# Sixteen transposes of the identity at four places, and the last product's activations 128 bytes lower

## The chip, the cores and the metric

The kernel runs on one core of a Trainium2 chip, alone. The metric is the device time of one execution, in microseconds (us). The median of three runs of the kernel before is 845.64 us (844.99 to 845.87). Weights are float32 in HBM; with the other inputs 139 MB are read. A core has TensorE (PE, matrix products; its weight loads are shown apart as PEld), VectorE (DVE), ScalarE (ACT), GpSimd (POOL) and SyncE (SP, which issues the weight transfers). TensorE multiplies a stationary operand, loaded first, with a moving operand that is streamed past it; here stationary blocks are 128 x 128, and 256 or 512 columns move.

## The reference, cut to what matters

Two transformer blocks on one sequence of 256 tokens with 1024 features. The first has a stick-breaking attention, an RWKV-7 mixer and a gated feed-forward of width 2816; the second a dilated attention with a short convolution, a cross attention to a memory of 256 rows, and a squared-ReLU feed-forward of width 4096.

```python
def first_block(x, ...):
    h = rms_norm(x, norm_mix_pre)                    # o_sb, o_rw, gates from h @ w_in
    x = x + rms_norm(merged @ w_o, norm_mix_post)
    h = rms_norm(x, norm_ffn_pre)
    f = (silu(h @ w_ffn_gate) * (h @ w_ffn_up)) @ w_ffn_down
    return x + rms_norm(f, norm_ffn_post)

def second_block(x, mem, ...):
    x = x + hybrid_mixer(rms_norm_2(x, g_mix), w_in, conv_w, g_attn_out, g_conv_out, w_out)
    x = x + memory_cross_attention(rms_norm_2(x, g_xattn), rms_norm_2(mem, g_mem), ...)
    x = x + squared_relu_mlp(rms_norm_2(x, g_mlp), w_up, w_down)
    return rms_norm_2(x, g_final)
```

## The kernel before, in words

**Products.** Weights come in slabs of 128 x 1024 elements (512 KB). For each slab SP issues a transfer into `wraw` (3 buffers), ACT rounds it to `whi` (4 buffers, L193) and DVE takes the rest, `wlo` (4 buffers, L194). The activations lie in memory as such a pair too (`xh`, `xl`; `yh`, `yl`; `fh`, `fl`; `ah`, `al`). A product of a 128 x 128 weight block with 256 tokens is three matmuls into one accumulator: hi with hi, weights' hi with activations' lo, weights' lo with activations' hi. A slab is 24 matmuls with 256 moving columns, one straight behind the other.

**Roles.** In most products the weights are stationary and the activations move (`block`, L258, written `mm<-xh,whi`: the moving operand stands first). In the groups with `tok` (the values of the memory, `kv(4)` to `kv(7)`, and two groups of `w_in_2`) and in the last product, `w_down_2`, it is the other way round: the activations are stationary and the weights move, in `w_down_2` with 512 columns at a time (`tokens`, L273).

**Places in memory.** A tile's byte address in its partition is set by the order of the pools, and `shift` (L121) puts a dummy tile of so many bytes ahead. In the built program `whi` and `wlo` lie at multiples of 512 bytes; `xh`, `xl`, `yh`, `yl`, `fh`, `fl`, the cross attention's output `xoh`, `xol` and the memory's `memh`, `meml` and keys `kT` at 192 modulo 512 (from `PHASE = 192`). `ah` and `al`, the stationary operand of `w_down_2`, lie at 320 modulo 512, behind a shift of 832 - 192 = 640 bytes.

**Sums of squares.** Each norm needs the sum of squares over the features, which is over partitions. `rstd_sum` makes it with one float32 matmul of a 128 x 128 tile of ones, `ssum` (two passes in the trace), into the first 256 columns of a PSUM bank; ACT then takes a logarithm and an exponential (L156). It is placed in the stream of products: for the first feed-forward behind the first four slabs (`together` calls `between` after the first block of each of four groups), for the dilated attention as the last step of the woven side work, for the convolution in `conv_norm`, ahead of `kv(4)`. Two other norms go through `rstd_tok` (one column for each token, `rtok`).

**Order.** Each engine takes its instructions in the order in which the code issues them. `together` runs the first halves (512 rows) of four groups, then `between`, then the second halves. `weave` runs one step of a generator ahead of each slab. Transposes go through TensorE as matmuls with the identity (`n.c("ident")`, 128 columns), as `turn` in `mlp`, `pt` in `hybrid` and `cross`, `tr` in the first block.

Of the kernel before, what the change touches and what calls it, by code (L numbers as in the profile page):

```python
# [17 lines left out]
P = 128  # L18
T = 256
D = 1024  # L20
# [12 lines left out]
PHASE = 192  # L33
# [59 lines left out]
class Net:  # L93
# [183 lines left out]
        self.nc.scalar.copy(hi, src)  # L277
        self.nc.vector.tensor_sub(lo, src, hi.bitcast(F32))

    def rstd(self, pool, src, width, tag):  # L280

        return self.rstd_sum(pool, [self.squares(pool, src)], width, tag)

    def sumsq(self, pool, s, acc):
        sq = pool.tile([P, 2, T], F32, tag="t2", name="sq", bufs=self.t2)
# [4 lines left out]
        self.nc.vector.tensor_add(a2, acc, sq)  # L290
        return a2

    def rstd_sum(self, pool, parts, width, tag, square=None):

        ps = self.ax("ssum")
        for i, p in enumerate(parts):
            self.mm(ps[:, :T], self.ones, p, start=i == 0)
        lg = pool.tile([P, T], F32, tag="t1", name="lg", bufs=1)
        r = pool.tile([P, T], F32, tag=tag, name=tag)
        self.act(lg, ps[:, :T], AF.Ln, bias=self.eps, scale=1.0 / width)  # L300
        self.act(r, lg, AF.Exp, scale=-0.5)
        if square is not None:
            self.act(square, lg, AF.Exp, scale=-1.0)
        return r
# [49 lines left out]
def staggered(count, *stages, apart=1):  # L354


    n = len(stages)
    for s in range(count + n - 1):
        for k, stage in zip(range(n - 1, -1, -1), stages):
            if 0 <= s - k < count:  # L360
                stage(s - k)
        for _ in range(apart):
            yield


def pair(t):
    return t.rearrange("p (o t) -> p o t", o=1).to_broadcast([P, 2, T])


def pairs(t):  # L370
    return [t[:, i:i + 2, :] for i in range(0, t.shape[1], 2)]
# [674 lines left out]
def plain_add(n, w, hi, lo, between=None):  # L1046

    for g, ps in enumerate(n.together([(w, g) for g in range(4)], hi, lo, between)):
        n.nc.vector.tensor_add(n.x[:, 2 * g:2 * g + 2, :], ps, n.x[:, 2 * g:2 * g + 2, :])


def ffn(n, tmp, wide, filler):
    nc, tc = n.nc, n.tc
    with tc.tile_pool(name="ffn", bufs=1, reuse_waits="tile") as pool:
        rs = []
        banks = n.together(FFN_FIRST, n.xh, n.xl, lambda: rs.append(
            pair(n.rstd_sum(tmp, [n.squares(tmp, pairs(n.x))], D, "rs"))))
        r = rs[0]
        n.table("silu_and_others")
        fh = pool.tile([P, FF // P, T], F32R, name="fh")  # L1060
        fl = pool.tile([P, FF // P, T], F32R, name="fl")
        for g in range(FF // 256):
            pg = banks[2 * g] if g < 2 else n.group("w_ffn_gate", g, n.xh, n.xl)
            s = tmp.tile([P, 2, T], F32, tag="t2", name="s", bufs=n.t2)
            nc.vector.tensor_mul(s, pg, r)
            n.act(s, s, AF.Silu)
            pu = banks[2 * g + 1] if g < 2 else n.group("w_ffn_up", g, n.xh, n.xl)
            m = tmp.tile([P, 2, T], F32, tag="t2", name="m", bufs=n.t2)
            nc.vector.tensor_mul(m, pu, r)
            nc.vector.tensor_mul(m, m, s)  # L1070
            n.split(m, fh[:, 2 * g:2 * g + 2, :], fl[:, 2 * g:2 * g + 2, :])
        n.table("natural_log_exp_and_others")
        branch_add(n, tmp, wide, "w_ffn_down", fh, fl, "norm_ffn_post", filler, "g_mix_2")
# [30 lines left out]
def hybrid(n, tmp, kv):  # L1104
    nc, tc = n.nc, n.tc
    with ExitStack() as ctx:
        pool = ctx.enter_context(tc.tile_pool(name="hyb", bufs=1, reuse_waits="tile"))
# [3 lines left out]
        rs = []  # L1111
# [16 lines left out]
        at = pool.tile([P, NP, T], F32, name="at")  # L1128
# [40 lines left out]

        def dilated():  # L1170
            yield from staggered(NP, values, turned, scores, apart=2)
            ra = n.rstd(tmp, pairs(at), 512, "ra")
            n.normed(tmp, pairs(at), ra, "g_attn_out_2", yh, yl)
            yield

        n.weave(dilated())
        for g in range(2):
            ps = n.group("w_in_2", 4 + g, n.xh, n.xl, tok=True)
# [6 lines left out]
        cv = pool.tile([P, NP, T], F32, name="cv")  # L1185
        nc.vector.memset(u[:, :, 0:2], 0.0)
        for g in range(2):
            ps = n.group("w_in_2", 6 + g, n.xh, n.xl)
            nc.vector.tensor_mul(bg[:, 2 * g:2 * g + 2, :], ps, r)
        for g in range(2):  # L1190
            ps = n.group("w_in_2", 8 + g, n.xh, n.xl)
            nc.vector.tensor_mul(cg[:, 2 * g:2 * g + 2, :], ps, pair(r2))
        for g in range(2):
            gg = slice(2 * g, 2 * g + 2)
            ps = n.group("w_in_2", 10 + g, n.xh, n.xl)
# [8 lines left out]
        n.unweave()  # L1204

        def conv_norm():
            rc = n.rstd(tmp, pairs(cv), 512, "rs")
            kv(4, n.ax("kv").rearrange("p (c t) -> p c t", c=2))
            n.normed(tmp, pairs(cv), rc, "g_conv_out_2", yh[:, NP:, :], yl[:, NP:, :])

        plain_add(n, "w_out_2", yh, yl, conv_norm)


def cross(n, tmp, kT, vm, kv):
    nc, tc = n.nc, n.tc
    with ExitStack() as ctx:
        pool = ctx.enter_context(tc.tile_pool(name="xat", bufs=1, reuse_waits="tile"))
        oh = pool.tile([P, KC, T], F32R, name="xoh")
        ol = pool.tile([P, KC, T], F32R, name="xol")
        n.scaled(pairs(n.x), "g_xattn_2", n.xh, n.xl)  # L1220
        rs = []
# [72 lines left out]
        n.weave(attention())  # L1294
        kv(6)
        kv(7)
        plain_add(n, "w_o_mem_2", oh, ol)
        n.unweave()


def mlp(n, tmp, out):
    nc, tc = n.nc, n.tc
    with ExitStack() as ctx:
        pool = ctx.enter_context(tc.tile_pool(name="mlp", bufs=1, reuse_waits="tile"))
        n.shift(pool, 832 - PHASE)
        ah = pool.tile([P, 32, T], F32R, name="ah")
        al = pool.tile([P, 32, T], F32R, name="al")
        n.scaled(pairs(n.x), "g_mlp_2", n.xh, n.xl)
        gf = pool.tile([P, D], F32, name="gf")
        r2 = pool.tile([P, 2], F32, name="r2")  # L1310
        xt = pool.tile([P, 2, D], F32, name="xt")

        def norm():
            n.rstd_tok(pool, [n.squares(tmp, pairs(n.x))], D, square=r2)

        def turned():

            for f in range(2):
                pt = n.ax("turn")
                for i in range(4):  # L1320
                    nc.tensor.transpose(pt[:, i * P:(i + 1) * P],
                                        n.v("g_final_2", 4 * f + i).to_broadcast([P, P]), n.c("ident"))
                nc.scalar.copy(gf[:, f * 512:(f + 1) * 512], pt)
                yield
            for t in range(2):
                for f in range(2):
                    pt = n.ax("turn")
                    for i in range(4):
                        nc.tensor.transpose(pt[:, i * P:(i + 1) * P],
                                            n.x[:, 4 * f + i, t * P:(t + 1) * P], n.c("ident"))  # L1330
                    nc.scalar.copy(xt[:, t, f * 512:(f + 1) * 512], pt)
                    yield

        banks = n.together([("w_up_2", g) for g in range(4)], n.xh, n.xl, norm)
        n.weave(turned())
        for g in range(16):
            ps = banks[g] if g < 4 else n.group("w_up_2", g, n.xh, n.xl)
            a = tmp.tile([P, 2, T], F32, tag="t2", name="a", bufs=n.t2)
            nc.scalar.activation(a, ps, AF.Relu)
            m = tmp.tile([P, 2, T], F32, tag="t2", name="m", bufs=n.t2)  # L1340
            nc.vector.scalar_tensor_tensor(m, ps, 0.0, a, op0=ALU.max, op1=ALU.mult)
            n.split(m, ah[:, 2 * g:2 * g + 2, :], al[:, 2 * g:2 * g + 2, :])
        n.unweave()
        o = pool.tile([P, 2, D], F32, name="o")
        st = pool.tile([P, 2, 4], F32, name="fst")
        for g in range(2):
            gg = slice(g * 512, (g + 1) * 512)
            for t, ps in enumerate(n.tokens("w_down_2", g, ah, al)):
                y = xt[:, t, gg]
                nc.vector.scalar_tensor_tensor(y, ps, r2[:, t:t + 1], y, op0=ALU.mult, op1=ALU.add)  # L1350
                sq = tmp.tile([P, 512], F32, tag="t2", name="sq", bufs=n.t2)
                nc.scalar.activation(sq, y, AF.Square, accum_out=st[:, t, g:g + 1])
                nc.vector.tensor_mul(o[:, t, gg], y, gf[:, gg])
        for t in range(2):
            s = st[:, t, :]
            nc.vector.tensor_add(s[:, 2:3], s[:, 0:1], s[:, 1:2])
            n.act(s[:, 3:4], s[:, 2:3], AF.Ln, bias=n.eps, scale=1.0 / D)
            n.act(s[:, 3:4], s[:, 3:4], AF.Exp, scale=-0.5)
            for f in range(2):
                oo = o[:, t, f * 512:(f + 1) * 512]  # L1360
                if f:
                    nc.vector.tensor_scalar(oo, oo, s[:, 3:4], None, op0=ALU.mult)
                else:
                    nc.scalar.activation(oo, oo, AF.Copy, scale=s[:, 3:4])
                nc.sync.dma_start(out[t * P:(t + 1) * P, f * 512:(f + 1) * 512], oo)
# [85 lines left out]
```

## Time and profile before

| what | value |
| --- | --- |
| median of 3 runs | 845.64 us |
| the profiled execution | 845.12 us |
| its span, first to last instruction | 843.4 us |
| PE busy | 818.9 us, 97% |
| PEld busy | 777.1 us, 92% |
| DVE, ACT busy | 565.0 us (67%), 464.5 us (55%) |
| DMA traffic | 142.88 MB, 169 GB/s mean |

The profiled execution's own time is 1.7 us above its span. PE is busy nearly everywhere, but its matmuls overlap (one is shown as 0.28 us long while the next begins 0.11 to 0.12 us after it), so the share of busy time doesn't tell how fast the products run; the distance between two starts does. Where the text below speaks of a pace, it is that distance, in ns.

### The profile page before, as it was taken

The page shows a single profiled execution, that of the slowest core. Times are in us where ns is not written, and L with a number is a line of the kernel's source. Part 1 is how long each engine was busy: PE and PEld are TensorE (multiplying, and loading weights), DVE is VectorE, ACT ScalarE, POOL GpSimd, SP SyncE. Part 2 cuts the span into 40 slices and gives each one's busy share as a digit, 9 for nine tenths or more (in the row PEclk, how much of TensorE's full clock was granted, in tenths as well). Part 3 has the DMA queues.
Part 4 walks back from the last instruction along what each step waited for, and adds up shares of the span by engine and source line. Part 5 has one row for each costly group of instructions (what it writes and reads, how often), then busy time and mean ns, then how long its engine had stood idle before and what let it go on. Part 6 is the DMA issues. An engine that isn't in the chain of part 4 may idle for free.

```text
span 843.4 us, 15763 instructions
## 1 busy us (share of the span) xinstructions
PE 818.9 (97%) x6508; PEld 777.1 (92%) x6508; DVE 565.0 (67%) x790; ACT 464.5 (55%) x714; POOL 5.7 (1%) x18
## 2 busy tenths in 40 slices
PE   5999998999999999999999999999999999999996
PEld 5898987999999999999999998999999999988884
DVE  6958689455978776666544876689676676654543
ACT  6587355643577654445444656457455575553432
POOL 0001001000000000000000000000000000000000
PEclk9999999999999999999999999999999999999998
DMA  8444433543464755555566464455534555555551
GB/s 289 141 150 152 141 127 119 163 148 99 136 245 147 228 189 185 194 181 191 167 192 184 155 209 146 147 180 193 179 100 155 194 177 178 198 188 186 194 181 51
DMA packets 44632, 142.88 MB, mean 169 GB/s; under 512 B 8977, under 2 KB 9745, under 8 KB 44305
## 3 DMA queue, kind: packets, MB, share of 16 engines
q1 hardware_dynamic: 43840, 139.25, 50.9%
q10 hardware_dynamic: 720, 2.63, 0.8%
q8 instruction: 51, 0.84, 0.4%
q14 instruction: 21, 0.16, 0.1%
HBM read 139.17 MB, written 2.69 MB: 168 GB/s over the span
## 4 chain that ended last, share of the span: by engine, by line
PE 81%; DVE 9%; ACT 4%; DMA 3%; issue 2%; DVEq 0%; ACTq 0%; SPq 0%
PE mm L258 59%; PE mm L273 11%; DVE wlo L194 3%; PE pz L273 2%; ACT whi L193 1%; DMA mraw<-in_mem 1%; PE rw L258 1%; PE po L273 1%; PE px L273 1%; PE mgnh L273 1%; PE ssum L273 1%; PE nv L273 1%; DVE prw L747 1%; PE kv L258 1%; DVE xl L326 1%
## 5 line engine op out<-in xcount | busy, mean ns | idle before, releaser
L194 DVE TENSOR_TENSOR wlo<-wraw,whi 128x1024 fp32r<-128x1024 f32 x254 | 308.2, 1215 | 191.0 <-ACT whi L193 190.2
L193 ACT CAST whi<-wraw 128x1024 fp32r<-128x1024 f32 x254 | 264.6, 1044 | 282.8 <-PE mm L258 162.5
L258 PE MATMUL mm<-xh,whi 128*128 128x256 f32 x1120 | 316.5, 283 | 0.0
L258 PE MATMUL mm<-xh,wlo 128*128 128x256 f32 x1120 | 313.4, 280 | 1.9 <-DVE wlo L194 1.9
L258 PE MATMUL mm<-xl,whi 128*128 128x256 f32 x1120 | 313.4, 280 | 0.0
L258 PEld LDWEIGHTS mm<-xh,wlo 128*128 128x128 f32 x1120 | 212.1, 189 | 3.2 <-DVE wlo L194 2.9
L258 PEld LDWEIGHTS mm<-xh,whi 128*128 128x128 f32 x1120 | 210.9, 188 | 3.7 <-issue 2.1
L258 PEld LDWEIGHTS mm<-xl,whi 128*128 128x128 f32 x1120 | 210.7, 188 | 0.9 <-issue 0.6
L273 PE MATMUL mm<-wlo,ah 128*128 128x512 f32 x128 | 50.6, 395 | 0.0
L273 PE MATMUL mm<-whi,al 128*128 128x512 f32 x128 | 50.6, 395 | 0.0
L273 PE MATMUL mm<-whi,ah 128*128 128x512 f32 x128 | 50.6, 395 | 0.0
L258 PE MATMUL mm<-fh,whi 128*128 128x256 f32 x176 | 49.5, 281 | 0.0
L258 PE MATMUL mm<-fl,whi 128*128 128x256 f32 x176 | 49.5, 281 | 0.0
L258 PE MATMUL mm<-fh,wlo 128*128 128x256 f32 x176 | 49.5, 281 | 0.0
L258 PEld LDWEIGHTS mm<-fh,wlo 128*128 128x128 f32 x176 | 33.8, 192 | 0.0
L258 PEld LDWEIGHTS mm<-fh,whi 128*128 128x128 f32 x176 | 33.0, 188 | 0.0
L258 PEld LDWEIGHTS mm<-fl,whi 128*128 128x128 f32 x176 | 33.0, 188 | 0.0
L273 PEld LDWEIGHTS mm<-whi,al 128*128 128x128 f32 x128 | 24.1, 188 | 5.8
L273 PEld LDWEIGHTS mm<-wlo,ah 128*128 128x128 f32 x128 | 24.1, 188 | 5.8
L273 PEld LDWEIGHTS mm<-whi,ah 128*128 128x128 f32 x128 | 24.1, 188 | 5.7
L258 PE MATMUL rw<-gh,whi 128*128 128x256 f32 x48 | 14.9, 310 | 8.6 <-ACT whi L193 8.6
L258 PE MATMUL mm<-memh,whi 128*128 128x256 f32 x64 | 18.5, 288 | 0.0
(352 smaller groups left out, 1377.4 us busy)
## 6 DMA issues: line engine op xcount, KB each, us to landing
wraw<-in_w_up SPq DMA_DIRECT2D x32, 512.0 KB, 3.3
wraw<-in_w_down SPq DMA_DIRECT2D x32, 512.0 KB, 3.3
wraw<-in_w_in SPq DMA_DIRECT2D x24, 512.0 KB, 4.1
wraw<-in_w_ffn_gate SPq DMA_DIRECT2D x22, 512.0 KB, 3.4
wraw<-in_w_ffn_up SPq DMA_DIRECT2D x22, 512.0 KB, 3.3
wraw<-in_w_ffn_down SPq DMA_DIRECT2D x20, 512.0 KB, 3.6
wraw<-in_w_gate SPq DMA_DIRECT2D x16, 512.0 KB, 3.3
wraw<-in_w_kv_mem SPq DMA_DIRECT2D x16, 512.0 KB, 3.3
```

Of the source, the lines that this page charges most:

```text
L193: nc.scalar.copy(hi[:, :w], raw[:, :w])
L194: nc.vector.tensor_sub(lo[:, :w], raw[:, :w], hi[:, :w].bitcast(F32))
L258: self.nc.tensor.matmul(ps[:, c, :], lhsT, rhs, start=first, stop=last, skip_group_check=True)
L273: self.nc.tensor.matmul(out, lhsT, rhs, start=start, stop=stop, skip_group_check=True)
L326: self.nc.vector.scalar_tensor_tensor(lo[:, k, :], s[:, j, :], g, hi[:, k, :].bitcast(F32), op0=ALU.mult, op1=ALU.subtract)
L747: nc.vector.tensor_mul(pr, left[:, r:r + 4, :].rearrange("p r (o i) -> p r o i", o=1).to_broadcast([P, 4, 16, 16]), right.rearrange("p (o ...
```

## The change

At three of the eight sums of squares, `rstd_sum` is called with `turned=True` and issues four transposes of the identity into the unused second half of the bank of the sum, behind its matmul. In the cross attention's output product, four such transposes go into a bank of their own between the first and the second halves. Nothing reads what they write. The shift in `mlp` is 512 bytes in place of 640, so `ah` and `al` (and `gf`, `xt`, `o` and others behind them) lie 128 bytes lower: `ah` and `al` at 192 modulo 512.

```diff
-    def rstd(self, pool, src, width, tag):
+    def rstd(self, pool, src, width, tag, turned=False):
 
-        return self.rstd_sum(pool, [self.squares(pool, src)], width, tag)
+        return self.rstd_sum(pool, [self.squares(pool, src)], width, tag, turned=turned)
...
+    def turns(self, ps):
+
+        for i in range(4):
+            self.nc.tensor.transpose(ps[:, T + i % 2 * P:T + (i % 2 + 1) * P], self.c("ident"), self.c("ident"))
+
-    def rstd_sum(self, pool, parts, width, tag, square=None):
+    def rstd_sum(self, pool, parts, width, tag, square=None, turned=False):
 
         ps = self.ax("ssum")
         for i, p in enumerate(parts):
             self.mm(ps[:, :T], self.ones, p, start=i == 0)
+        if turned:
+            self.turns(ps)
...
-            pair(n.rstd_sum(tmp, [n.squares(tmp, pairs(n.x))], D, "rs"))))
+            pair(n.rstd_sum(tmp, [n.squares(tmp, pairs(n.x))], D, "rs", turned=True))))
...
-            ra = n.rstd(tmp, pairs(at), 512, "ra")
+            ra = n.rstd(tmp, pairs(at), 512, "ra", turned=True)
...
-            rc = n.rstd(tmp, pairs(cv), 512, "rs")
+            rc = n.rstd(tmp, pairs(cv), 512, "rs", turned=True)
...
-        plain_add(n, "w_o_mem_2", oh, ol)
+        plain_add(n, "w_o_mem_2", oh, ol, lambda: n.turns(n.ax("turns")))
...
-        n.shift(pool, 832 - PHASE)
+        n.shift(pool, 512)
```

On PE in the first feed-forward, at the sum behind the first four slabs (`xh` is the activations, `whi` and `wlo` the weights, `sqa` the squares, `mm_3225` the first group's accumulator, back for its second half), before:

```order
L258 MATMUL mm_3228<-xl_77,whi_3260 128x256
L258 MATMUL mm_3228<-xh_76,wlo_3261 128x256
L273 MATMUL ssum_3364<-sqa_3361,ones_61 128x256 [waits DVE_49]
L258 MATMUL mm_3225<-xh_76,whi_3290 128x256 [waits Activation_49]
L258 MATMUL mm_3225<-xl_77,whi_3290 128x256
```

and after:

```order
L258 MATMUL mm_3228<-xl_77,whi_3260 128x256
L258 MATMUL mm_3228<-xh_76,wlo_3261 128x256
L273 MATMUL ssum_3364<-sqa_3361,ones_61 128x256 [waits DVE_49]
L296 MATMUL ssum_3364<-cst_58 128x128 x4
L258 MATMUL mm_3225<-xh_76,whi_3290 128x256 [waits Activation_49]
```

The four transposes stand between the sum and the next product and wait for nothing of their own; the same holds at the two other sums. On PE in the cross attention's output product, between its first and second halves (`xoh`, `xol` the activations), before:

```order
L258 MATMUL mm_7441<-xol_6863,whi_7497 128x256
L258 MATMUL mm_7441<-xoh_6862,wlo_7498 128x256
L258 MATMUL mm_7438<-xoh_6862,whi_7527 128x256
L258 MATMUL mm_7438<-xol_6863,whi_7527 128x256
L258 MATMUL mm_7438<-xoh_6862,wlo_7528 128x256
```

and after:

```order
L258 MATMUL mm_7453<-xol_6875,whi_7509 128x256
L258 MATMUL mm_7453<-xoh_6874,wlo_7510 128x256
L296 MATMUL turns_7613<-cst_58 128x128 x4
L258 MATMUL mm_7450<-xoh_6874,whi_7539 128x256
L258 MATMUL mm_7450<-xol_6875,whi_7539 128x256
```

Four transposes more, and nothing else moved: the rows of the other engines, and what each of them waits on, are the same in both programs.

## Rows read from the trace of the kernel before

**Rows 1.** The page: span, busy TensorE, granted clock in 40 slices (tenths).

```profile
span 843.4 us, 15763 instructions
...
PE 818.9 (97%) x6508; PEld 777.1 (92%) x6508; DVE 565.0 (67%) x790; ACT 464.5 (55%) x714; POOL 5.7 (1%) x18
...
PEclk9999999999999999999999999999999999999998
```

**Rows 2.** The page: the chain that ended last, by engine and by line.

```profile
PE 81%; DVE 9%; ACT 4%; DMA 3%; issue 2%; DVEq 0%; ACTq 0%; SPq 0%
PE mm L258 59%; PE mm L273 11%; DVE wlo L194 3%; PE pz L273 2%; ACT whi L193 1%; DMA mraw<-in_mem 1%; PE rw L258 1%; PE po L273 1%; PE px L273 1%; PE mgnh L273 1%; PE ssum L273 1%; PE nv L273 1%; DVE prw L747 1%; PE kv L258 1%; DVE xl L326 1%
```

**Rows 3.** Windows, PE: stretch, sum, busy (x matmuls), granted clock, DMA share, GB/s.

```profile
290.00:460.00 170.00, 170.00 (x1445) 1.00 0.59 186
546.00:567.00 21.00, 21.00 (x181) 1.00 0.58 186
569.00:573.50 4.50, 4.50 (x40) 1.00 0.62 217
575.00:596.00 21.00, 21.00 (x180) 1.00 0.62 198
645.00:666.00 21.00, 21.00 (x180) 1.00 0.52 176
695.00:745.00 50.00, 50.00 (x444) 1.00 0.58 192
747.00:833.00 86.00, 86.00 (x370) 1.00 0.50 164
```

**Rows 4.** Timeline of PE, first feed-forward: start us, duration us, instruction; its last product.

```profile
288.10 0.28 PE L258 MATMUL mm<-xh,wlo 128*128 128x256 f32 x1
288.22 0.59 PE L273 MATMUL ssum<-sqa,ones 128*128 128x256 f32 x2
288.46 0.47 PE L258 MATMUL mm<-xh,whi 128*128 128x256 f32 x1
288.77 0.28 PE L258 MATMUL mm<-xl,whi 128*128 128x256 f32 x1
288.88 0.28 PE L258 MATMUL mm<-xh,wlo 128*128 128x256 f32 x1
...
463.78 0.28 PE L258 MATMUL mm<-fh,wlo 128*128 128x256 f32 x1
```

**Rows 5.** Timeline of PE: the last transposes of `mlp`, and `w_up_2` behind them.

```profile
693.72 0.28 PE L258 MATMUL mm<-xh,wlo 128*128 128x256 f32 x1
693.84 0.60 PE L1329 MATMUL turn<-cst,x 128*128 128x128 f32 x4
694.20 0.36 PE L258 MATMUL mm<-xh,whi 128*128 128x256 f32 x1
...
694.51 0.28 PE L258 MATMUL mm<-xh,wlo 128*128 128x256 f32 x1
...
745.87 0.28 PE L258 MATMUL mm<-xh,wlo 128*128 128x256 f32 x1
```

**Rows 6.** Windows, PE: just ahead of transposes in the first block, and behind them.

```profile
55.00:64.00 9.00, 9.00 (x78) 1.00 0.60 198
65.60:68.50 2.90, 2.90 (x28) 1.00 0.51 171
```

**Rows 7.** Timeline of PE, cross attention: where the stationary operand changes.

```profile
609.53 0.28 PE L258 MATMUL mm<-whi,meml 128*128 128x256 f32 x1
...
610.10 0.28 PE L258 MATMUL mm<-whi,memh 128*128 128x256 f32 x1
...
629.64 0.28 PE L258 MATMUL mm<-xoh,whi 128*128 128x256 f32 x1
...
630.35 0.28 PE L258 MATMUL mm<-xoh,whi 128*128 128x256 f32 x1
```

**Rows 8.** Waits of ACT: who waited for whom, us in total, times, longest.

```profile
ACT whi L193 <- PE mm L258: 162.5, 116, 4.7
```

## The prediction, on record before the kernel ran

> **What bounds the kernel now.** I read the page first: PE is busy for 97% of the 843.4 us, at the granted clock's full level (2.4 GHz) in every slice but the last [rows 1]; the chain of waits is 81% PE, and 70% of it are the slab products on two lines [rows 2]. So the kernel ends when its products end, and the question is how fast one follows the other. Weights don't limit that: ACT waits 162.5 us in all for PE to give back a `whi` buffer [rows 8], so slabs stand ready ahead of PE.
>
> Then I took the distance between starts from the timeline of PE, and found **two paces** for the same matmul at the same clock. Behind the sum of squares of the first feed-forward, 1486 steps lie between 288.77 and 463.78 us (62 slabs' worth, 1488 matmuls, counted from the second) [rows 4]: 175.01 / 1486 = 117.8 ns. Behind the last transposes of `mlp`, 453 steps lie between 694.51 and 745.87 (19 slabs, 456 matmuls, counted from the third) [rows 5]: 51.36 / 453 = 113.4 ns. Shape, roles and places modulo 512 are the same in both. The windows show that a pace lasts until something interrupts the products: 1445 matmuls in 170 us, 181 in 21, 180 in 21, 180 in 21 are all the slow one, 444 in 50 us is the fast one (a window counts the two that began just ahead of it, too) [rows 3]. The difference is 4.4 ns a matmul.
>
> What chooses the pace is the restart. The slow stretches that the change is about begin behind a sum of squares or, in the cross attention, behind a value product. Four or more 128-column transposes straight ahead of products are followed by the fast pace in all ten places of this trace that are long enough to tell (at 65, 72, 532 and 634 us, and six within `mlp`), also where the pace ahead of them was slow: 78 in 9 us before, 28 in 2.9 us after [rows 6], which is 118 and 112 ns without the two early ones. Without transposes the restart goes either way.
>
> **The change part by part.**
>
> A. The first feed-forward. If the four transposes leave the products at the fast pace up to the next sum at 463.9 us, 1484 steps gain 4.4 ns each: 6.5 us. Cost: four transposes and the restart behind them. In `mlp`, the transposes take 693.84 to 694.20, 0.36 us, and the restart to the third product's start 0.31 us [rows 5]; the sum's own restart, which now falls away, takes 288.46 to 288.88, 0.42 us [rows 4]. That adds 0.36 + 0.31 - 0.42 = 0.25 us; the step from the sum's second pass to the first transpose isn't in the trace and may cost up to the sum's own restart gap, 0.31 - 0.12 = 0.19 us more. I take 0.35, the middle of 0.25 to 0.45. Net: 6.2 us less. Weights can follow: `w_up_2` runs the fast pace on the same slabs with 192 GB/s against 186 now [rows 3]. The sum's readers on ACT wait at most those 0.4 us longer; DVE needs their result a slab later, PE (through a bank that DVE frees) four slabs later.
>
> B. The dilated attention's sum. Its stretch runs slow from 545 to 568 us [rows 3], 190 steps: 0.84 - 0.35 = 0.5 us less.
>
> C. The convolution's sum. Behind it come 48 matmuls of `kv(4)`, activations stationary (40 in 4.5 us, slow), then 192 with the weights stationary (180 in 21 us, slow) [rows 3]. The only place where such a change of roles met the fast pace without an interruption lost it: from 629.64 to 630.35 six steps take 0.71 us, 118 ns [rows 7]. So I count 46 steps, 0.2 us, against 0.35: 0.15 us more. If the pace holds it is 238 steps, 1.05 - 0.35 = 0.7 us less.
>
> D. The cross attention. The transposes stand alone, at slow pace, with 192 slow matmuls behind them (180 in 21 us) [rows 3]: 0.85 us gained. In `mlp` three steps with transposes between take 693.72 to 694.51, 0.79 us, where three plain ones take 0.34 [rows 5]: 0.45 us. Net 0.4 us less.
>
> E. The last product. It runs 370 matmuls in 86 us [rows 3], 233 ns for 512 columns (1.7 began early). No row shows this product with its operands elsewhere; the bounds come from the 256-column rows doubled: twice the fast pace is 226.7 ns, twice the slow one 235.5. So today's 233.3 is near the slow pace. The place moves the stationary operand to 192 modulo 512 with the moving one at 0, the same relation as in `kv(6)`; there the products come out of a fast stretch (their moving operand at 192, too) and stay fast: from 609.53 to 610.10 five steps in 0.57 us, 114 ns [rows 7]. The last product follows a fast stretch in the same way [rows 5]. I take the fast value, by that nearest row: 383 x (233.3 - 226.7) = 2.5 us less. The ends kept for the range: if a matmul's excess over 512 columns at 2.4 GHz (213.3 ns) is no larger than the fast pace's over 256 (113.4 - 106.7 = 6.7 ns), 220 ns, 5.1 us less; twice the slow pace, 0.8 us more.
>
> Sum: 6.2 + 0.5 - 0.15 + 0.4 + 2.5 = 9.45 us less. The profiled execution took 845.12 us, 0.5 us under the median of the runs: 845.12 - 9.45 = 835.7, and against the median 845.64 - 9.45 = **836.2 us**. Nothing of it is given back later: what DVE and ACT do behind each of these stretches starts from PE's results.
>
> A page speaks against A to E at once. The Trainium skill, "TensorE: Matmul & The Clock Gate", Part 2, says that loading the next weights doesn't take read bandwidth from the running matmul; by that rule neither a restart nor a place in memory could set the pace, and only the costs would remain. The trace disagrees as far as it goes, with 117.8 and 113.4 ns for one shape at one clock [rows 4, 5].
>
> **The rivals.**
>
> R1. The last product's place does nothing (its pace is set within its first steps, not by the place): A to D stay, E is 0: 838.7 us. For it: its start already follows a fast stretch and is slow all the same [rows 3, 5]. Against: the relation of the operands there is another than in `kv(6)`.
>
> R2. The pace is lost on the way. In A it must hold over 62 slabs and the change from `xh` to `fh`; the fast stretch of `mlp` held over 19 [rows 5]. Lost halfway, A gives 2.9 instead of 6.2: 839.5 us with E, 842.0 without.
>
> R3. The sum, not the transposes, sets the pace, or the pace isn't chosen by restarts at all (this is also what the page's rule would make of it): A to D cost 3 x 0.35 + 0.45 = 1.5 us and give nothing. 847.1 us, or 844.6 with E. For it: no row has a sum and transposes in a row. Against: a slow stretch ahead of transposes didn't matter [rows 6].
>
> R4. The other side: the new place hurts the last product. Moving and stationary operand meet at the change of roles at the same place modulo 512, and if each of the 384 weight loads then holds up its matmul, it costs 384 times the stall. It decides from 9.45 - 2.5 = 6.95 us, 18 ns a matmul, a pace over 251 ns. The nearest row is 4.4 ns a weight load (slow against fast), a quarter of it; at 25 ns it would be 838.7 + 9.6 = 848.3 us.
>
> **How the numbers follow.** Forecast 0.45; R1 0.22; R2 0.15; R3 0.13 (0.06 with E, 0.07 without); R4 0.05. About 0.2%, 1.7 us, is what a measurement of this kernel can tell from no change: 843.9 to 847.3. Faster: forecast, R1, R2 and a little of R3, 0.84; same: R3, 0.11; slower: R4 and the worst of R3, 0.05. The range: its low end takes E at 220 ns, 836.2 - 2.6 = 833.6, and C held would lie there too; the high end takes R1 and R2 in, 842.0. R3 and R4 are left out.
>
> **What would show it.** In the changed kernel's timeline: behind the first feed-forward's transposes 24 matmuls take 2.72 us, not 2.83, up to 457 us or so (A); the same at 539 to 560 (B) and behind the cross attention's transposes (D); behind `kv(4)` the pace goes back to 118 (C); the last product's 370 matmuls take 84 us, not 86 (E). The three sums' restarts are 0.25 to 0.45 us longer. I am wrong if the pace behind sum and transposes is 118 ns, if the fast pace breaks at a slab whose weights came late, or if the last product's distance isn't between 220 and 235.5 ns.

## The result, and the profile after

The changed kernel takes 837.15 us (median of 4 runs, 835.33 to 838.26) against 845.32 us before (4 runs, 844.06 to 845.87): a ratio of 0.9906, interval 0.9889 to 0.9923, some 8 us less. 836.2 us was forecast, in a range of 833.6 to 842.0. The profiled execution took 837.66 us, its span 835.9.

The page of the changed kernel answers to [rows 1]. It still shows a PE at 97% and the full clock; only the sum of PE's busy time is smaller:

```profile
span 835.9 us, 15795 instructions
...
PE 811.8 (97%) x6524; PEld 771.9 (92%) x6524; DVE 564.8 (68%) x790; ACT 465.7 (56%) x714; POOL 5.7 (1%) x18
...
PEclk9999999999999999999999999999999999999999
```

The windows show where; columns as in [rows 3], stretches moved along with the products:

```profile
291.00:455.00 164.00, 164.00 (x1450) 1.00 0.61 193
541.00:562.00 21.00, 21.00 (x188) 1.00 0.56 190
563.50:568.00 4.50, 4.50 (x40) 1.00 0.61 222
570.00:590.00 20.00, 20.00 (x179) 1.00 0.61 200
640.00:660.00 20.00, 20.00 (x179) 1.00 0.55 180
592.00:602.00 10.00, 10.00 (x87) 1.00 0.58 202
662.00:672.00 10.00, 10.00 (x87) 1.00 0.58 197
689.00:739.00 50.00, 50.00 (x444) 1.00 0.59 191
742.00:826.00 84.00, 84.00 (x369) 1.00 0.51 166
```

The first feed-forward now has 1450 matmuls in 164 us where it had 1445 in 170; the stretches B and D and the one behind `kv(4)` are fast, too (188 in 21 us for 181, 179 in 20 us for 180 in 21). `kv(4)` itself stays slow, 40 in 4.5 us. The last product has 369 in 84 us for 370 in 86. `w_up_2` behind its transposes is as it was, 444 in 50 us. Two stretches have become slow, which no row ahead of the prediction speaks of: 87 matmuls in 10 us at 592 and 662 us. In the kernel before, the same two ran fast:

```profile
598.00:607.00 9.00, 9.00 (x82) 1.00 0.54 187
...
668.00:677.00 9.00, 9.00 (x82) 1.00 0.57 192
```

The start of the same instruction in the two traces tells where the time went. A row's last column is what its stretch, from the row above, brought:

| instruction on PE | before, us | after, us | difference | change since the row above |
| --- | --- | --- | --- | --- |
| sum of the first feed-forward | 288.22 | 289.19 | +0.97 | +0.97, same code in both |
| sum behind `w_ffn_down` | 463.90 | 458.71 | -5.19 | -6.16 (A) |
| sum of the dilated attention | 544.98 | 539.68 | -5.30 | -0.11 |
| sum of the convolution | 568.02 | 562.32 | -5.70 | -0.40 (B) |
| `rtok` in `w_q_mem_2` | 596.72 | 590.62 | -6.10 | -0.40 (C) |
| first scores of the cross attention | 608.05 | 602.37 | -5.68 | +0.42 |
| its last value product | 639.75 | 634.08 | -5.67 | +0.01 |
| `rtok` in `w_up_2` | 666.61 | 660.54 | -6.07 | -0.40 (D) |
| first transposes in `mlp` | 677.94 | 672.29 | -5.65 | +0.42 |
| first step of the last product | 745.99 | 740.33 | -5.66 | -0.01 |
| its last step | 835.34 | 827.99 | -7.35 | -1.69 (E) |
| end of the span | 843.42 | 835.93 | -7.49 | -0.14 |

The restart of A, to be held against [rows 4]:

```profile
289.07 0.28 PE L258 MATMUL mm<-xh,wlo 128*128 128x256 f32 x1
289.19 0.59 PE L273 MATMUL ssum<-sqa,ones 128*128 128x256 f32 x2
289.62 0.60 PE L296 MATMUL ssum<-cst 128*128 128x128 f32 x4
289.98 0.37 PE L258 MATMUL mm<-xh,whi 128*128 128x256 f32 x1
290.18 0.28 PE L258 MATMUL mm<-xl,whi 128*128 128x256 f32 x1
290.30 0.28 PE L258 MATMUL mm<-xh,wlo 128*128 128x256 f32 x1
```

From the last product ahead of the sum to the third one behind it are 1.23 us where it was 0.78: the four transposes cost 0.45 us here.

### The profile page after: what moved, and what is told of

It is laid out like the page before. It is cut to its first block, busy times and chain, and to the rows that moved or that the text cites. A ratio compares the mean times of both kernels' runs of the same rounds, so it can differ in the third digit from the quotient of the medians.

```text
span 835.9 us, 15795 instructions
## 1 busy us (share of the span) xinstructions
PE 811.8 (97%) x6524; PEld 771.9 (92%) x6524; DVE 564.8 (68%) x790; ACT 465.7 (56%) x714; POOL 5.7 (1%) x18
## 4 chain that ended last, share of the span: by engine, by line
PE 84%; DVE 7%; ACT 4%; DMA 3%; issue 1%; SPq 0%; ACTq 0%; DVEq 0%
PE mm L258 60%; PE mm L273 11%; PE rw L258 2%; DVE wlo L194 2%; PE pz L273 2%; ACT whi L193 1%; PE po L273 1%; PE px L273 1%; DMA mraw<-in_mem 1%; DMA wraw<-in_w_rw 1%; PE mgnh L273 1%; PE nv L273 1%; PE kv L258 1%; DMA wraw<-in_w_sb 1%; DVE pr L736 1%
```

## The experiments

**Each half of the change alone.** First the transposes without the new place:

```diff
-        n.shift(pool, 512)
+        n.shift(pool, 832 - PHASE)
```

> The sixteen transposes alone; ah and al stay at 320 modulo 512. Theory T (four transposes restart the products at the fast pace): the first feed-forward takes 113.4 ns a matmul as in the changed kernel, the last product stays at 233 ns; the difference of the two traces at its start, 5.7 us, is what the transposes bring, so 845.3 - 5.7 = 839.6 us. Rival P (the place in memory brings it all, the feed-forward's pace is chance of a run): 845 us, 118 ns in the feed-forward.

Measured: 836.34 us against 844.14 before on that chip, ratio 0.9903 (0.9867 to 0.9939). The windows of the first feed-forward and of the last product:

```profile
288.00:452.00 164.00, 164.00 (x1450) 1.00 0.60 193
740.00:824.00 84.00, 84.00 (x362) 1.00 0.50 163
```

The feed-forward is fast, and the last product is at its old pace (362 in 84 us, 233 ns). Theory T holds here, rival P doesn't. Ahead of the sum the products ran fast already in this execution (91 in 10 us):

```profile
276.00:286.00 10.00, 10.00 (x91) 1.00 0.78 238
```

So this run alone doesn't show that the transposes turn a slow stream fast; the profile of the changed kernel does, where the products ahead are slow, and in the probes below a single sum ended every fast stretch that it met. The 7.8 us are more than the 5.7 expected; the profiled execution had gained 1.9 us on that of before by 288 us, where the two programs are still the same, so part of it is chance.

Then the place without the transposes:

```diff
-        n.shift(pool, 832 - PHASE)
+        n.shift(pool, 512)
```

> The place alone (ah and al at 192 modulo 512), no added transposes. Theory T with the place as its own cause: the feed-forward stays at 118 ns, the last product goes from 233.3 to 228.9 ns, 383 x 4.4 ns = 1.7 us less: 843.6 us. Rival (the last product's pace is set by how the stretch ahead of it runs, and the place does nothing): 233 ns, 845.3 us.

Measured: 842.23 us, ratio 0.9975 (0.9959 to 0.9992). First feed-forward and last product:

```profile
291.00:461.00 170.00, 170.00 (x1446) 1.00 0.58 186
749.00:832.00 83.00, 83.00 (x365) 1.00 0.51 165
```

The feed-forward is slow, the last product has its new pace: between its first and its last start lie 383 steps in 87.67 us (746.37 to 834.04), 228.9 ns. So the place acts by itself, and the two halves add up within their intervals (0.9903 x 0.9975 = 0.9878 against 0.9906).

**How many transposes?** The changed kernel with one at each place:

```diff
-        for i in range(4):
+        for i in range(1):
             self.nc.tensor.transpose(ps[:, T + i % 2 * P:T + (i % 2 + 1) * P], ...
```

> The changed kernel with one transpose in place of four at each of the four places. Theory T in its simplest form (what stands last ahead of the products decides): fast pace as with four, and 12 transposes of 108 ns less, 1.3 us: 837.2 - 1.3 = 835.9 us. Rival (it takes several to empty the queue of weight loads): 118 ns in the feed-forward, and only the place's 1.7 us stay: about 844 us.

Measured: 840.46 us, ratio 0.9937 (0.9908 to 0.9965), and nine executions between 834.18 and 842.69 us. In the profiled one the feed-forward and B stayed slow; D became fast, and so did `kv(4)` (113.3 ns), which had stayed slow behind four transposes. Feed-forward, B and D:

```profile
288.00:458.00 170.00, 170.00 (x1446) 1.00 0.57 186
544.00:565.00 21.00, 21.00 (x181) 1.00 0.58 185
643.00:663.00 20.00, 20.00 (x179) 1.00 0.56 184
```

So neither was right: one transpose falls either way. That some executions reach 834 and some 842 fits a feed-forward that is fast in some and slow in others, though only one was profiled.

**Is it the transposes, or any further work?** In the kernel before, the sum of the first feed-forward a second time instead:

```diff
         if turned:
-            self.turns(ps)
+            self.mm(ps[:, T:], self.ones, parts[-1], start=False)
```

> The kernel before with one edit: behind the first feed-forward's sum, in place of four transposes, the float32 matmul of ones with the squares a second time, into the unused half of the bank (nothing reads it). It holds the products up by 0.43 us, as long as the four transposes (0.45). Theory T (the kind of the last instruction decides): the restart is that of a sum, 305 ns, then 118 ns: 845.3 + 0.4 = 845.7 us. Rival U (any further work or delay at this place shifts the products into the fast pace): 113.4 ns, 839.3 us.

Measured: 837.13 us in the single run. Here is the restart, four passes of a float32 matmul with the old gap of 0.31 us behind it, the windows ahead of it and behind:

```profile
286.62 0.28 PE L258 MATMUL mm<-xh,wlo 128*128 128x256 f32 x1
286.73 1.02 PE L273 MATMUL ssum<-sqa,ones 128*128 128x256 f32 x4
287.40 0.47 PE L258 MATMUL mm<-xh,whi 128*128 128x256 f32 x1
287.71 0.28 PE L258 MATMUL mm<-xl,whi 128*128 128x256 f32 x1
```

```profile
276.00:286.50 10.50, 10.50 (x94) 1.00 0.83 236
289.00:453.00 164.00, 164.00 (x1450) 1.00 0.60 193
```

Theory T in the form "transposes restart fast, sums restart slow" falls: two sums gave the whole gain. But the stretch ahead was fast as well in this execution, by chance, where it is slow in the profile of before (88 in 10 us):

```profile
278.00:288.00 10.00, 10.00 (x88) 1.00 0.71 217
```

So I formed T2, that the restart as a whole picks the pace, with some sequences sure and others not, and put it against mere chance and against a pace that is kept or turned over.

**Many restarts in one run.** Two kernels throw something in ahead of each of 18 groups of 48 matmuls of the first feed-forward, in the kernel before:

```diff
+        def probe():
+            kind, count = next(kinds)
+            pp = n.ax("probe")
+            for _ in range(count):
+                if kind == "s":
+                    n.mm(pp[:, :T], n.ones, n.x[:, 0, :])
+                else:
+                    nc.tensor.transpose(pp[:, :P], n.c("ident"), n.c("ident"))
```

> The kernel before, with something thrown in ahead of each of the 18 groups from the third on (48 matmuls each) of the first feed-forward's gate and up products, into a bank that nothing reads, in this order three times over: one sum (two passes), four transposes, two sums, one transpose, eight transposes, two transposes. Theory T2 (the restart picks the pace; four transposes always pick the fast one, one sum the slow one, and the others fall by where they happen to stand): all six groups behind four or eight transposes at 113.4 ns, all three behind one sum at 118, the rest mixed. Rival C (the pace is chance at every restart): four transposes and one sum mixed as well. Rival D (the pace ahead is kept or turned over): fast and slow go by the group before, not by the kind.

> As the probe before, in another order twice over: four transposes, one sum, four transposes, one sum, two transposes, two sums, one transpose, two sums, one transpose. T2: all four groups behind four transposes at 113.4 ns, all four behind one sum at 118 although each stands behind a fast group; the five other kinds mixed. Rival C: mixed everywhere. Rival D: a sum behind a fast group leaves it fast.

Measured, from the starts of a group's fourth to its last product (44 steps), every group is at 113.3 to 113.4 ns or at 117.7 to 117.8, none between:

| thrown in | pace ahead | fast in the first kernel | fast in the second |
| --- | --- | --- | --- |
| one sum | fast | 0 of 2 | 0 of 3 |
| one sum | slow | 0 of 1 | 0 of 1 |
| two sums | fast | 3 of 3 | 1 of 1 |
| two sums | slow | none | 0 of 3 |
| one transpose | fast | 0 of 3 | 0 of 1 |
| one transpose | slow | none | 1 of 3 |
| two transposes | slow | 3 of 3 | 1 of 2 |
| four transposes | slow | 3 of 3 | 3 of 4 |
| eight transposes | slow | 0 of 3 | none |

Two places of the second kernel, both with four transposes behind a slow group that a single sum had started; the first fast, the second slow:

```profile
313.23 0.29 PE L258 MATMUL mm<-xh,wlo 128*128 128x256 f32 x1
313.36 0.60 PE L1071 MATMUL probe<-cst 128*128 128x128 f32 x4
...
314.03 0.28 PE L258 MATMUL mm<-xh,wlo 128*128 128x256 f32 x1
314.15 0.28 PE L258 MATMUL mm<-xh,whi 128*128 128x256 f32 x1
...
319.13 0.28 PE L258 MATMUL mm<-xh,wlo 128*128 128x256 f32 x1
...
367.25 0.29 PE L258 MATMUL mm<-xh,wlo 128*128 128x256 f32 x1
367.38 0.60 PE L1071 MATMUL probe<-cst 128*128 128x128 f32 x4
...
368.05 0.28 PE L258 MATMUL mm<-xh,wlo 128*128 128x256 f32 x1
368.17 0.28 PE L258 MATMUL mm<-xh,whi 128*128 128x256 f32 x1
...
373.35 0.28 PE L258 MATMUL mm<-xh,wlo 128*128 128x256 f32 x1
```

In the first, 45 steps from the third product take 319.13 - 314.03 = 5.10 us; in the second, 5.30. T2 holds for one sum (slow in all seven, whatever the pace ahead). For transposes it fails as stated: four are fast in six of seven, and eight, which it had fast, are slow in all three. Two sums go by rival D: they kept the pace that was there, seven times in seven, which also fits the run with the sum twice. Pure chance (rival C) doesn't fit, since in the first kernel each kind came out alike all three times. What these sequences do to the products that follow is thus regular in part, and none of the theories gives all of it.

The same kernel once more, in more executions:

> The second sum in the first feed-forward once more, in rounds. In the probes two sums in a row were followed by the fast pace in four of seven places. If which pace they pick depends on how the stream happens to stand there: executions that differ by 6 us, some near 837 and some near 844 us. If it is fixed at this place: all near 837 us.

Measured: 838.24 us, ratio 0.9921 (0.9900 to 0.9943), its four executions between 837.99 and 838.93 us, all near 837 as expected for a pace that is fixed at this place. Again the stretch ahead was fast in the profiled one (95 in 10.5 us):

```profile
277.00:287.50 10.50, 10.50 (x95) 1.00 0.74 237
290.00:454.00 164.00, 164.00 (x1449) 1.00 0.60 193
```

That leaves a second reading: two sums keep the pace ahead, as in the probes, and it was fast each time. Of the fourteen traces of this study seven are fast ahead of this place and seven slow; three more fast ones by chance (in the executions without a profile) would come, as an estimate, one time in eight. The times don't decide between the two.

**Other places for the last product.** The changed kernel with one number changed:

```diff
-        n.shift(pool, 512)
+        n.shift(pool, 576)
```

> The changed kernel with ah and al at 256 modulo 512 (shift 576). If the last product's pace is a matter of the place alone: its own steady value over all 383 steps, between the 228.9 ns at 192 and the 233.3 at 320, 231 by the middle, +0.8 us. Rival (192 is special, because the moving operand ahead stands there too): 233 ns or more.

and with 768 in place of 576:

> The changed kernel with ah and al at 448 modulo 512 (shift 768). By a place's own value, further from 192 than 320 is: 233 ns or more, +1.7 us or more; by a pattern that repeats every 256 bytes, as 192: 228.9 ns, no change.

Measured in one execution each (833.69 and 835.90 us; at 843.85 the kernel before on that chip): the windows of the last product, at 256 modulo 512 and, second, at 448:

```profile
740.00:822.00 82.00, 82.00 (x363) 1.00 0.50 167
```

```profile
742.00:824.00 82.00, 82.00 (x360) 1.00 0.50 167
```

By the starts of its 384 matmuls: 226.7 ns at 256 (737.07 to 823.89 us), 228.9 at 448 (738.61 to 826.27), against 228.9 at 192 and 233.3 at 320. Each place has its own steady value, the same in every execution with it that I compared (four traces at 192, six at 320, three at 256; one alone at 448). My guess of 231 at 256 was wrong; 448 does repeat 192, but what was expected beyond that, a pattern in 256 bytes, would put 320 beside 64, which wasn't tried.

**The changed kernel, the best place, and two transposes.** Three kernels on one chip, with 844.46 us for the kernel before: the changed kernel, the same with 256, and that with two transposes.

```diff
-        for i in range(4):
+        for i in range(2):
             self.nc.tensor.transpose(ps[:, T + i % 2 * P:T + (i % 2 + 1) * P], ...
...
-        n.shift(pool, 512)
+        n.shift(pool, 576)
```

> The changed kernel once more, to stand beside the next one on the same chip: 0.9906 of the kernel before, about 836.5 us; the first feed-forward fast (113.4 ns), the last product at 228.9 ns.

> The changed kernel with ah and al at 256 modulo 512, in rounds. The single look had the last product at 226.7 ns, twice the fast pace of 256 columns. If the pace is the place's own: 226.7 again, 383 x 2.2 ns = 0.8 us less than the changed kernel beside it. If it was chance of that execution: no difference.

> As the kernel before it in this list (256 modulo 512), with two transposes in place of four at the four places. They were followed by the fast pace in four of five places of the probes, and cost 0.22 us less at each place. If two are enough in these places: 0.9 us less than with four. If they fall either way, as one does: executions that differ by 6 us, some at 833 and some at 839 to 840 us, the mean no better than with four.

| kernel | median us | ratio to before | interval |
| --- | --- | --- | --- |
| the change | 835.72 | 0.9888 | 0.9867 to 0.9910 |
| with 256 modulo 512 | 834.65 | 0.9878 | 0.9855 to 0.9901 |
| and two transposes | 832.62 | 0.9853 | 0.9835 to 0.9871 |

The step to 256 can't be told from none by the times; the pace shows it (226.7 ns). Two transposes were fast in A, B and D of the profiled execution, and its four executions lie between 832.07 and 833.09 us, with none 6 us off. Its feed-forward and last product:

```profile
288.00:452.00 164.00, 164.00 (x1450) 1.00 0.58 191
738.00:820.00 82.00, 82.00 (x364) 1.00 0.50 167
```

This version is faster than both kernels of the study: 0.9853 against 0.9888 for the change on the same chip; the two intervals overlap a little, but its slowest execution (833.09 us) is below the fastest of the change (834.00). Worked out were 0.8 us for the place and 0.9 for the transposes; the 3.1 us between the medians are more. In the two profiled executions, 1.9 us apart, 1.0 us is there at the first feed-forward's sum already (286.14 against 285.14 us), ahead of which the programs are the same; what makes the rest between the medians stays open.

## Why the prediction was right

**What bounds the kernel**: confirmed. With no engine's work changed but 16 matmuls added, the end moved by 7.5 us, and by the table of starts it was the products' pace that moved it: 8.5 us from the first feed-forward's sum on, net of what the transposes cost, less the 0.97 that this execution was behind there.

**A** (6.2 us forecast) brought 6.16. The fast pace held over all 62 slabs: from 290.18 to 458.60 us are 1486 steps of 113.3 ns. R2 fell, and so did R3: the products ahead of the sum were slow in this execution, as before the change, and those behind the transposes fast. The window ahead:

```profile
279.00:289.00 10.00, 10.00 (x87) 1.00 0.71 224
```

Six traces of this study have the sum and four transposes in A and in B. The products behind were fast in all twelve places; those ahead were slow in seven of them and fast in five. The cost was 0.45 us, the upper end of 0.25 to 0.45: the unseen step from the sum's second pass to the first transpose is the long one.

**B** (0.5) and **D** (0.4) brought 0.40 each.

**C** was forecast at 0.15 us more and brought 0.40 less. The step that failed is that `kv(4)` would run fast behind its sum and transposes: it stayed slow, 40 in 4.5 us, in all six traces with four transposes there. So four transposes aren't followed by the fast pace everywhere, not even within the changed kernel; that A, B and D are such places was right, but the rule behind it ("in all ten places of this trace") is narrower than the prediction took it, as the eight transposes of the probe show, too. The change of roles behind `kv(4)` then met the slow pace instead of the fast one, and the products behind it were fast (179 in 20 us). At the place of [rows 7] in the cross attention the same change turned the pace over in all fourteen traces: from fast to slow in eleven, from slow to fast in three. One of the three is the run with 448 modulo 512; fourth and last product of either role:

```profile
619.66 0.28 PE L258 MATMUL mm<-whi,memh 128*128 128x256 f32 x1
622.01 0.28 PE L258 MATMUL mm<-wlo,memh 128*128 128x256 f32 x1
...
622.48 0.28 PE L258 MATMUL mm<-xoh,whi 128*128 128x256 f32 x1
624.75 0.28 PE L258 MATMUL mm<-xoh,wlo 128*128 128x256 f32 x1
```

20 steps take 2.35 us, then 20 take 2.27. So the row was read rightly for a fast pace; nothing told what a slow one would do. Behind `kv(4)` it stayed slow in the six traces that have no transposes there, so this isn't a rule for every change of roles either. That C came out on the good side is luck.

**E** had the right sign and mechanism, and its size was off: the term "twice the fast pace, 226.7 ns" measured 228.9, so 1.7 us instead of 2.5. R1 fell with the place alone (228.9 ns, ratio 0.9975). What the nearest row gave, 226.7, is the value at another place, 256.

**Left out of the sum**: "nothing of it is given back later". Of what came back, two pieces of 0.42 us each are the stretches at 592 and 662 us. Each stands behind an `rtok` that B to D left alone. Before, the products ahead of it were slow and those behind it fast; now those ahead are fast and those behind slow. In all fourteen traces of this study each of the 28 restarts behind these two sums turned the pace over, 16 from fast to slow and 12 from slow to fast. So a fast stretch was bought twice at the price of the next one, 94 steps x 4.4 ns. And the changed kernel's profiled execution was 0.97 us behind at 288 us already, by stretches in which the programs are the same.

The sum went 9.45 us; measured were 7.5 between the spans, 8 between the medians. The misses of E (0.8 too much), the two turned stretches (0.84) and the start of the execution (0.97) are more than the difference, and C, better by 0.55, makes up for part of it by luck.

**The rule of the page.** The Trainium skill, "TensorE: Matmul & The Clock Gate", Part 2, says that loading the next weights doesn't take read bandwidth from the running matmul. What the prediction drew from it, that neither a restart nor a place in memory could set the pace, isn't borne out: the place of the stationary operand alone moved the last product from 233.3 to 228.9 ns, with its weight loads shown as 188 ns long at both places. Whether the load takes reads from the running matmul or acts on it in another way, no run here shows.

## What to carry to other kernels

In a kernel that is bound by back-to-back matmuls, take the distance between two starts, stretch by stretch, before anything else: busy share and clock were the same at two paces 4% apart. A short interruption can be worth far more than it costs if thousands of matmuls follow at the pace that it leaves; try a few kinds and counts at the very place, since one transpose, two, four and eight did different things here, and look at what the next interruption turns over. Where the stationary operand is an activation tile, its place in memory is worth a sweep: it is one number.

## What the runs showed of the hardware that was not expected

Weight load and matmul of the same shapes, at one clock, have two stable paces, 113.3 and 117.8 ns for 256 columns, and no third one in 36 restarts of the probes. Behind sums, transposes and probes the pace is steady from the sixth product on at the latest. Which one follows depends on the sequence ahead. In the probes, one float32 sum of two passes was always followed by the slow one (7 of 7), two sums by the one that was there ahead (7 of 7), eight transposes by the slow one (3 of 3, each time with the same kinds ahead of them), four mostly by the fast one (6 of 7). The four passes of `rtok` with one column each, where they stand alone, turned the pace over in 28 of 28. These counts are of this kernel's places and no rule for every place: at 16 us a single sum of two passes was followed by the fast pace in two of the fourteen traces, and `kv(4)` was slow behind four transposes. With 512 columns the pace goes by the place of the stationary operand: 226.7 ns at 256 modulo 512, 228.9 at 192 and 448, 233.3 at 320, the weights that move at 0. What inside the chip makes the two paces stays open: the traces show starts to the nanosecond and nothing of the reads.
